# Early gate blocks two at a time in two banks, and the scores of a head's first two query blocks issued as one group

## The chip, the cores and the metric

One core of a Trainium2 chip runs the whole layer. The metric is the device time of one execution in microseconds (us), the median of several runs. The engines are named as the profile names them: PE is the matrix engine (PEld its weight loads), DVE the vector engine, ACT the scalar engine, POOL the GpSimd engine, SP the engine whose queue issues the DMAs.

## What is computed

One decoder layer on x of 1024 tokens by 1024 features, all in float32:

```python
h = rms_norm(x, norm_w)
proj = h @ w_in                                   # 1024 x 11296
q, k, v, z_a, xbc, z_s, dt_raw, gate_logits = split(proj)
# branch A: 8 heads, two softmax maps each, causal
p = softmax(where(causal, rms(q) @ rms(k).T / 8, -inf))
y_a = rms((p[0] - lam * p[1]) @ v) * silu(z_a)
# branch B: depthwise conv (4 taps) + silu on xbc, chunked state-space scan
# (32 heads, 4 groups, 8 chunks of 128), grouped rms norm of y * silu(z_s)
y_s = gated_group_rms_norm(ssd_chunked(...), z_s)
g_a, g_s = split(gate_logits)                     # 1024 + 1024
merged = sigmoid(g_a) * (y_a @ w_proj_attn) + sigmoid(g_s) * (y_s @ w_proj_ssd)
out = x + merged @ w_out
```

## The kernel before

Every large product is done in three matmuls of a reduced float format: each operand is split into a high and a low part (ACT rounds the high part, DVE or POOL subtracts it from the original to get the low part), and high x high, high x low and low x high add up in one PSUM bank. A weight tile is called `w` or, in a pair, `wp`; the two parts of the transposed h are `hH` and `hL`. There are eight PSUM banks, handed out by the slot list `trs`.

The program is written by a planner. Each piece of work is a Python generator; `Plan` keeps a modelled clock for PE (`pl.t`) and for each other engine, and always resumes the generator that is due first. The order of the instructions on each engine is the order in which the generators emit them. So a changed constant, modelled cost or table of order shifts instructions on all engines, while each engine executes its own in the written order and waits by semaphore for what is not ready.

The stages follow each other like this. **Front**: the table `FRONT_ORDER` is worked through item by item. `y0`, `y1` (tiles `pmz`) and `z..` (tiles `pz`) compute z_s; `c..` (tiles `fXc`, `fYc`, `fZc`) compute two column blocks of xbc each and their conv; `g..` (`fXg`, `fYg`, `fZg`) compute two column blocks of the gate logits; `d0` (`pdt`) computes dt. Items c, g and z are written as seven block products instead of eight; they read sums of blocks of h, the forms t1 to t4 (tiles `ft`), which ACT, DVE and POOL make from h during the first 100 us, and sums of weight blocks, which POOL makes (`rawf<-rawf,rawf`, `s<-rawf,rawf`) out of four raw tiles that have to be loaded together. The seven products of an item come in the order b11, t2, b21, t3, t1, t4, b22.

An `e` item (tile `pe`, function `gate_first`) computes the first 512 tokens of one gate block before the forms exist: 12 matmuls for the first half of the contraction, a copy of that partial sum by ACT (`gc`), which the later `g` item of the same number reads back from memory and then needs only five products, and 12 more matmuls into the same bank. The second 12 overwrite nothing, but PE has to wait for the copy before it adds to the bank. In the old order there are four `e` items (e6, e0, e4, e2), and each runs on its own.

**Attention and scan**: after the front come eight heads (`att_proj`, tiles `pma`, 192 matmuls each); the scan's chunks (`px`, `pc`, `pb`, `pS`, `pO`, `pD`, `py`) and the softmax blocks of the heads are woven in by the planner, a new chunk every `PACE` modelled us. The scores of a query block (`sc`, function `att_block`) contract over 64 rows: two maps are computed side by side on the two row halves of the array, three matmuls each, so a group is six matmuls; query block qb has 128 x (qb + 1) columns, in pieces of at most 512. `att_core` starts the four blocks of a half head one after the other, `SPACE` modelled us apart, and `STACK` sets how long after the last projection of the half the transposes of q and k are due. The intra-chunk products of the scan (`pO` or `pD`, output 64 x 64) use the array in column halves. `TURN` is the modelled cost of a change between such shapes.

**End**: the last four gate blocks (`pg`), then three block products with the projection weights (`px`, `py`, `pz` with `wp`), then the output product (`po..`).

`NEARLY` and `WPOOL` say for which weight tiles the low part is computed on POOL instead of DVE: from tile number `NEARLY` on, every `WPOOL`-th. `ZSUMS` sets when weight sums for z (`os`) are due.

Of the kernel before, what the change touches and what calls it, by code (L numbers as in the profile page):

```python
# [15 lines left out]
P = 128  # L16
S = 1024
D = 1024
KB = D // P
# [12 lines left out]
C_DT = 9216  # L32
C_GATE = 9248
NBIG, NW, NRAW, NMID, NSM = 17, 9, 4, 16, 8
PACE = 18.0
FRONT = 12
SLOW = 32.0
FRONT_ORDER = "y0 e6 y1 e0 e4 c6 e2 d0 c20 z06 c16 z07 z05 g0 c2 z04 c0 c10 z16 z03 g2 z17 z15 c4 z14 z13 c8 c14 g6 g8 c12 g4 g10 c22 c18"
REST = (("t2", 6), ("b22", 3), ("t3", 7), ("t1", 5), ("t4", 4))
ZSUMS = (75.0, 182.0, 3.0)  # L40
WPOOL = 3
NEARLY = 48
FINAL = (("b11", 1), ("t1", 5), ("t2", 6), ("t3", 7), ("b21", 2), ("b22", 3), ("t4", 4))
NFIN = 4 * len(FINAL)
HOP = 0.12
DONE = 0.2
STACK = 2.0
SPACE = 0.4
AHEAD = 0.2
DLAG = 1.5  # L50
TURN = 0.089
# [101 lines left out]
def tile_hybrid_layer(ctx: ExitStack, tc: tile.TileContext, x, norm_w, w_in, q_norm_w, k_norm_w,  # L153
# [35 lines left out]
    heads, abb = Share(bigs, 8), Share(bigs, 1)  # L189

    def bigt(shape, dt=F32, name="b"):
        return big.tile(shape, dt, tag="b4", name=name)
# [10 lines left out]
    def trt(name):  # L203
        return ps_tr.tile([P, 512], F32, tag="tr", name=name)
# [11 lines left out]
    def mm(o, lhsT, rhs, start, stop, after=0.0, **kw):  # L216
        nc.tensor.matmul(o, lhsT=lhsT, rhs=rhs, start=start, stop=stop, **kw)  # L217
# [16 lines left out]
    def pe_done():  # L234
        return pl.t + DONE
# [153 lines left out]
    PAIR_C = {"c": C_XBC, "g": C_GATE}  # L389
    for kind, i in ORDER1:  # L390
        if kind in PAIR_C:
            if kind == "g" and ("e", i) in ORDER1:
# [202 lines left out]
    def w_next(n):  # L595
        i = used[0]
        used[0] += n
        return list(range(i, i + n))

    def w_need(i):  # L600
        while i not in w_at:
            yield pl.t + 0.1
        while w_at[i] > pl.t:
            yield w_at[i]
# [285 lines left out]
            trs.give(k, t1)  # L890
        pl.spawn(att_core(h, half, (q, kq)), max(done))

    def att_core(h, half, q):
        for qb in range(half * 4, half * 4 + 4):
            while bigs.avail(1 + half) > pl.t:
                a = bigs.avail(1 + half)
                yield a if a < INF else pl.t + 0.2
            pk = [bigs.take() for _ in range(1 + half)]
            pl.spawn(att_block(h, qb, pk, q))
            yield pl.t + SPACE  # L900

    def att_block(h, qb, pk, q):
        v, zg, kk, ks = hd[h]
        q, kq = q
        n = (qb + 1) * P
        qsl = slice(qb % 4 * P, (qb % 4 + 1) * P)
        ex = []
        if qb < 4:
            pboth = bigt([P, 2, 512], name=f"p{h}{qb}")

        def soft(m):
            p = bigt([P, S], name=f"p{h}{qb}{m}") if qb >= 4 else pboth[:, m]
            nms, t1 = [], 0.0
            for i, (j, e) in enumerate(cols):
                while len(scs) <= i:
                    yield pl.t + 0.1
                sc, k, at = scs[i]
                at = max(at, t1 - HOP)
                yield at
                nms.append(tin(1, "nm"))  # L920
                nc.vector.tensor_tensor_reduce(out=p[:, j:e], in0=sc[m][:, 0:e - j], in1=maskb[:, S - n + j:S - n + e],  # L921
                                               scale=-1.0, scalar=nms[i - 1] if i else 3e38, op0=ALU.add, op1=ALU.min,
                                               accum_out=nms[i])
                t1 = pl.op("V", 0.08 + 1.042e-3 * (e - j), at)
                trs.give(k[m], t1)
# [6 lines left out]
        cols, scs, got = [(j, min(n, j + 512)) for j in range(0, n, 512)], [], {}  # L932
        for j, e in cols:
            k = yield from pl.get(trs, 2)
            sc = [trt(f"sc{h}{qb}{m}{j}") for m in range(2)]
            for n3, (a, b) in enumerate(((0, 0), (0, 1), (1, 0))):
                for m in range(2):
                    ms = slice(m * 64, m * 64 + 64)
                    mm(sc[m][:, 0:e - j], q[ms, a, qsl], kk[b][ms, j:e], n3 == 0, n3 == 2)
            scs.append((sc, k, pe_done()))  # L940
            if j == 0:
                for m in range(2):
                    pl.spawn(soft(m), pe_done())
        if qb % 4 == 3:
            bigs.give(kq, pl.t + 0.1)
        while len(ex) < 2:
            yield pl.t + 0.3
        pr, sums = zip(*[got[m] for m in range(2)])
# [240 lines left out]
            w_done(ids[n])  # L1189
            pl.spawn(step(b, p, into[p], cell, *how), pe_done())  # L1190

    g_c, g_first = {}, {i for kind, i in ORDER1 if kind == "e"}

    def gate_first(b):
        ids = w_next(2)
        k = yield from pl.get(trs, first=True)
        pm = mmt(f"pe{b}")
        for half in range(2):
            yield from w_need(ids[half])
            while half and ("g", b) not in g_c:  # L1200
                yield pl.t + 0.1
            for kb in range(half * 4, half * 4 + 4):
                yield from steps3(pm, blk(ids, kb), (hH[:, kb, 0:512], hL[:, kb, 0:512]), kb == 0, kb % 4 == 3, skip_group_check=True)
            w_done(ids[half])
            if half:
                pl.spawn(gate_evac(b, 0, pm, k), pe_done())
            else:
                pl.spawn(gate_copy(b, pm), pe_done())

    def gate_copy(b, pm):  # L1210
        at = pe_done()
# [1022 lines left out]
```

## Time and profile before

| what | us |
|---|---|
| runs | 1562.31, 1562.57, 1564.35 |
| median | 1562.57 |
| the profiled execution | 1562.57, its span 1560.8 |
| PE busy in it | 1540.5 |
| DVE, ACT, POOL busy | 1146.5, 894.3, 774.9 |

The profile shows one execution. A row of its timeline gives the start, the time until the end, the engine, the source line, the operation with output and inputs, the tile shape, and how many equal instructions were merged; in brackets stands the idle time before it and what ended it. Since nearly all matmuls go through one helper, all have the line L217, and tiles are told apart by name. Matmuls overlap: the distance between the starts of two of them says more about the cost of one than its own duration.

### The profile page before, as it was taken

What the parts mean: (1) busy time and instruction counts of PE and PEld (TensorE: products, weight loads), DVE (VectorE), ACT (ScalarE), POOL (GpSimd) and SP (SyncE); (2) the same over time, 40 slices, a digit from 0 to 9 for tenths busy, and PEclk for the clock granted to TensorE, in tenths of its full rate; (3) what the DMA queues carried; (4) which work ended last, traced back from release to release, by engine and by line L of the source; (5) the groups of instructions that cost most, each with busy time, mean ns of one, the idle gap of its engine ahead of it and who ended that gap; (6) DMA issues with size and microseconds to landing.
All of it is one profiled execution on the core that took longest, in us unless ns stands there. A gap on an engine that the chain in (4) does not pass through costs nothing.

```text
span 1560.8 us, 26193 instructions
## 1 busy us (share of the span) xinstructions
PE 1540.5 (99%) x8562; PEld 1252.8 (80%) x8562; DVE 1146.5 (73%) x2113; ACT 894.3 (57%) x2207; POOL 774.9 (50%) x900
## 2 busy tenths in 40 slices
PE   7999999999999999999999999999999999999999
PEld 5777888888888888888878888787878888888887
DVE  6778867757786587777777677776555577898985
ACT  7653435466566566666676677676556565352350
POOL 3274365344554544546586556464647745222005
PEclk9999999999999999999999999999999999999999
DMA  6576696876445542424454424253437598698846
GB/s 229 165 243 204 228 303 209 270 233 212 146 157 148 154 145 96 140 71 136 159 180 139 136 82 136 75 159 99 162 115 224 194 338 291 229 340 269 301 135 223
DMA packets 257130, 291.66 MB, mean 187 GB/s; under 512 B 18647, under 2 KB 162784, under 8 KB 256994
## 3 DMA queue, kind: packets, MB, share of 16 engines
q1 hardware_dynamic: 256990, 289.99, 57.3%
q8 instruction: 68, 1.11, 0.3%
q14 instruction: 68, 0.56, 0.1%
q10 hardware_dynamic: 4, 0.00, 0.0%
HBM read 198.57 MB, written 91.36 MB: 186 GB/s over the span
## 4 chain that ended last, share of the span: by engine, by line
PE 95%; DMA 1%; ACT 1%; DVE 1%; issue 0%; POOL 0%; SPq 0%; DVEq 0%; ACTq 0%; POOLq 0%
PE pma L217 23%; PE pz L217 11%; PE py L217 6%; PE fYc L217 6%; PE sc L217 4%; PE av L217 4%; PE fXc L217 4%; PE px L217 4%; PE fZc L217 4%; PE pO L217 3%; PE pg L217 3%; PE fYg L217 3%; PE pmz L217 2%; PE pa L231 2%; PE poz L217 1%; PE fZg L217 1%
## 5 line engine op out<-in xcount | busy, mean ns | idle before, releaser
L217 PE MATMUL pma<-w,hH 128*128 128x512 f32 x1024 | 344.9, 407 | 0.0
L217 PEld LDWEIGHTS pma<-w,hH 128*128 128x128 f32 x1024 | 186.2, 189 | 40.8 <-issue 6.6
L217 PE MATMUL pma<-w,hL 128*128 128x512 f32 x512 | 207.9, 406 | 0.0
L248 ACT ACTIVATE w<-raw 128x512 fp32r<-128x512 f32 (+1 forms) x166 | 100.9, 631 | 57.2 <-DMA raw<-wf_d 21.1
L256 DVE TENSOR_TENSOR w<-raw,w 128x512 fp32r<-128x512 f32 (+1 forms) x136 | 107.3, 808 | 29.0 <-ACT w L248 28.2
L217 PEld LDWEIGHTS pma<-w,hL 128*128 128x128 f32 x512 | 96.7, 189 | 20.3 <-issue 2.9
L217 PE MATMUL fYc<-ft,wp 128*128 128x512 f32 x432 | 106.1, 392 | 2.4 <-DVE ft L256 1.8
L248 ACT ACTIVATE p<-p,nm 128x256 f32<-128x256 f32 (+7 forms) x128 | 98.1, 770 | 17.8 <-DVE nm L921 15.9
L256 POOL TENSOR_TENSOR rawf<-rawf,rawf 128x512 f32<-128x512 f32 x54 | 71.8, 1329 | 64.2 <-issue 20.6
L217 PEld LDWEIGHTS fYc<-ft,wp 128*128 128x128 f32 x432 | 80.4, 188 | 20.4 <-DVE ft L256 2.2
L921 DVE CUSTOM_DVE_ANT_0 p<-sc,maskb 128x512 f32<-128x512 f32 (+3 forms) x128 | 69.3, 586 | 29.8 <-PE sc L217 28.3
L248 ACT ACTIVATE wp<-rawp 128x512 fp32r<-128x512 f32 x72 | 44.2, 627 | 81.7 <-PE py L217 23.5
L217 PE MATMUL pz<-w,ft 128*128 128x512 f32 x384 | 90.5, 392 | 0.3 <-DVE w L256 0.3
L256 POOL TENSOR_TENSOR os<-os,os 128x512 f32<-128x512 f32 x48 | 65.1, 1357 | 43.0 <-DMA os<-in_w_out_dram 19.5
L217 PEld LDWEIGHTS pz<-w,ft 128*128 128x128 f32 x384 | 71.6, 188 | 15.4 <-DVE w L256 0.7
L256 POOL TENSOR_TENSOR rawp<-rawp,rawp 128x512 f32<-128x512 f32 x36 | 53.2, 1491 | 53.8 <-DVE wp L256 40.1
L248 ACT ACTIVATE ab<-ab,nac 128x128 f32<-128x128 f32 x256 | 78.4, 397 | 2.2 <-POOL ab L1486 2.1
L217 PEld LDWEIGHTS av<-v,at 128*128 128x128 f32 x576 | 72.5, 191 | 5.1 <-issue 1.1
L288 POOL TENSOR_TENSOR rs<-rs,mhalf 128x4 f32<-128x4 f32 (+1 forms) x71 | 73.6, 1036 | 5.9
L248 ACT ACTIVATE wp<-rawf 128x512 fp32r<-128x512 f32 x100 | 60.3, 623 | 27.6 <-POOL rawf L256 24.1
L217 PE MATMUL av<-v,at 128*128 128x128 f32 x576 | 75.4, 276 | 0.0
L217 PE MATMUL sc<-kk,q 64*128 64x512 f32 (+3 forms) x576 | 70.8, 366 | 0.0
(367 smaller groups left out, 4144.6 us busy)
## 6 DMA issues: line engine op xcount, KB each, us to landing
raw<-in_w_in_dram SPq DMA_DIRECT2D x104, 256.0 KB, 3.2
rawf<-in_w_in_dram SPq DMA_DIRECT2D x72, 256.0 KB, 4.3
ab<-act_d SPq DMA_DIRECT2D x32, 512.0 KB, 4.7
wf_d<-os SPq DMA_DIRECT2D x48, 256.0 KB, 5.4
cv_d<-cv SPq DMA_DIRECT2D x48, 256.0 KB, 2.7
raw<-wf_d SPq DMA_DIRECT2D x48, 256.0 KB, 3.1
t_d<-ts SPq DMA_DIRECT2D x24, 512.0 KB, 2.6
os<-in_w_in_dram SPq DMA_DIRECT2D x32, 256.0 KB, 4.3
```

Source lines behind the costliest of these rows:

```text
L217: nc.tensor.matmul(o, lhsT=lhsT, rhs=rhs, start=start, stop=stop, **kw)
L231: nc.tensor.transpose(out=o, in_=i, identity=ident if idn is None else idn)
L248: nc.scalar.activation(o, i, f, **kw)
L256: (nc.vector if eng == "V" else nc.gpsimd).tensor_tensor(out=o, in0=a, in1=b, op=op)
L288: nc.gpsimd.tensor_tensor(out=dst, in0=dst, in1=mhalf[:, 0:cols], op=ALU.pow)
L921: nc.vector.tensor_tensor_reduce(out=p[:, j:e], in0=sc[m][:, 0:e - j], in1=maskb[:, S - n + j:S - n + e], scale=-1.0, scalar=nms[i - 1] if ...
```

## The change

Six things are changed together.

1. `FRONT_ORDER` has two `e` items instead of four. Each now does two gate blocks, b and b + 2, in two banks: first half of b, first half of b + 2, second half of b, second half of b + 2. The copy of b's partial sum by ACT falls in the time of the matmuls of b + 2. The weight list has the four tiles in the same order.
2. The front's table is reordered: the item right behind the second `e` item is now g8, then c6 and d0; before it was c6, then e2 and d0. The set of blocks computed is the same.
3. In `att_core` the scores of query blocks 0 and 1 are written together, twelve matmuls in a row, into one bank per map (block 0 in columns 0 to 127, block 1 in 128 to 383); the bank is given back when both blocks have been read. Blocks 2 and 3 follow without the distance `SPACE`.
4. The planner counts a change of shape as 0.189 or 0.159 instead of 0.089 modelled us, and `STACK` is 3.5 instead of 2.0.
5. `PACE` is 17.5 instead of 18.0; `ZSUMS` is moved.
6. `WPOOL` is 2 instead of 3 and `NEARLY` 39 instead of 48: in the whole program 52 weight tiles get their low part from POOL instead of 30, and 114 instead of 136 from DVE.

```diff
-PACE = 18.0
+PACE = 17.5
-FRONT_ORDER = "y0 e6 y1 e0 e4 c6 e2 d0 c20 z06 c16 z07 z05 g0 c2 z04 c0 c10 z16 z03 g2 z17 z15 c4 z14 z13 c8 c14 g6 g8 c12 g4 g10 c22 c18"
+FRONT_ORDER = "y0 e4 y1 e0 g8 c6 d0 c20 z06 c16 z07 c10 g0 c2 z05 z04 c0 z16 g6 z03 g2 z17 c4 z15 z13 z14 c8 c14 g4 c12 g10 c18 c22"
-ZSUMS = (75.0, 182.0, 3.0)
-WPOOL = 3
-NEARLY = 48
+ZSUMS = (83.0, 185.0, 9.0)
+WPOOL = 2
+NEARLY = 39
+HBUF = 8
-STACK = 2.0
+STACK = 3.5
...
-        c += TURN * (now != shape[0])
+        if now != shape[0]:
+            c += TURN + 0.1 if "r" in now + shape[0] else TURN + 0.07
...
         elif kind == "e":
-            wlist += block_w(w_in, KB, C_GATE + i * P)
+            for q in range(2):
+                for b in (i, i + 2):
+                    wlist.append(block_w(w_in, KB, C_GATE + b * P)[q])
...
+    def att_core(h, half, qk):
+        q, kq = qk
+        kk = hd[h][2]
+        for qbs in (((4,), (5,), (6,), (7,)) if half else ((0, 1), (2,), (3,))):
...
+            if len(qbs) == 2:
+                pieces = [[(0, 0, P, 0), (1, 0, 2 * P, P)]]
+            else:
+                pieces = [[(qbs[0], j, min(n, j + 512), 0)] for j in range(0, n, 512)]
+            for piece in pieces:
+                k = yield from pl.get(trs, 2)
+                sc = [trt(f"sc{h}{qbs[0]}{m}{piece[0][1]}") for m in range(2)]
+                users = [len(piece)] * 2
+                for qb, j, e, o in piece:
+                    qsl = slice(qb % 4 * P, (qb % 4 + 1) * P)
+                    for i, (a, b) in enumerate(((0, 0), (0, 1), (1, 0))):
+                        for m in range(2):
+                            ms = slice(m * 64, m * 64 + 64)
+                            mm(sc[m][:, o:o + e - j], q[ms, a, qsl], kk[b][ms, j:e], i == 0, i == 2, skip_group_check=True)
+                    cells[qb].append((sc, k, pe_done(), o, users))
+            if half:
+                yield pl.t + SPACE
...
     def gate_first(b):
-        ids = w_next(2)
-        k = yield from pl.get(trs, first=True)
-        pm = mmt(f"pe{b}")
+        ids = w_next(4)
+        pms = []
+        for g in (b, b + 2):
+            k = yield from pl.get(trs, first=True)
+            pms.append((mmt(f"pe{g}"), k))
         for half in range(2):
...
+            for n, (pm, k) in enumerate(pms):
+                g, i = b + 2 * n, ids[2 * half + n]
+                yield from w_need(i)
+                while half and ("g", g) not in g_c:
+                    yield pl.t + 0.1
```

How this moves instructions is seen at three places. The first is PE at the first `e` item (`pe6` and `pe4` are the banks of gate blocks 6 and 4, `w8` to `w10` weight tiles in order of use). Before:

```order
L217 MATMUL pe6_576<-hH_114,w8_381 128x512 x2
L217 MATMUL pe6_576<-hL_115,w8_381 128x512
L217 MATMUL pe6_576<-hH_114,w8_381 128x512
L217 MATMUL pe6_576<-hH_114,w9_488 128x512
L217 MATMUL pe6_576<-hL_115,w9_488 128x512
```

Now:

```order
L218 MATMUL pe4_576<-hH_114,w8_381 128x512
L218 MATMUL pe6_577<-hH_114,w9_488 128x512
L218 MATMUL pe6_577<-hL_115,w9_488 128x512
L218 MATMUL pe6_577<-hH_114,w9_488 128x512 x2
L218 MATMUL pe6_577<-hL_115,w9_488 128x512
L218 MATMUL pe6_577<-hH_114,w9_488 128x512 x2
L218 MATMUL pe6_577<-hL_115,w9_488 128x512
L218 MATMUL pe6_577<-hH_114,w9_488 128x512 x2
L218 MATMUL pe6_577<-hL_115,w9_488 128x512
L218 MATMUL pe6_577<-hH_114,w9_488 128x512
L218 MATMUL pe4_576<-hH_114,w10_510 128x512
```

The second half of a block used to stand right behind its first half; now the twelve matmuls of the other block stand between them.

The second place is PE at the scores of head 2 (`sc2000` and `sc2010` are the two maps of query block 0, `sc2100` and `sc2110` of block 1). Before:

```order
L217 MATMUL sc2000_8378<-kk20_7542,q20_8265 128x128
L217 MATMUL sc2010_8379<-kk20_7542,q20_8265 128x128
L217 MATMUL pma26_8371<-w100_6424,hH_114 128x512
L217 MATMUL pma26_8371<-w100_6424,hL_115 128x512
L231 MATMUL px22_8401<-ident_99,xr22_8326 128x128 x4
L217 MATMUL pma26_8371<-w101_7431,hH_114 128x512 x2
L217 MATMUL pma26_8371<-w101_7431,hL_115 128x512
L217 MATMUL pma26_8371<-w102_7463,hH_114 128x512
L217 MATMUL pO21_8293<-xdt21_8087,ab21_8122 64x64 x16
L217 MATMUL sc2100_8444<-kk20_7542,q20_8265 128x256
L217 MATMUL sc2110_8445<-kk20_7542,q20_8265 128x256
```

Now:

```order
L218 MATMUL sc2000_8297<-kk20_7499,q20_8218 128x128
L218 MATMUL sc2010_8298<-kk20_7499,q20_8218 128x128
L218 MATMUL sc2000_8297<-kk20_7499,q20_8218 128x256
L218 MATMUL sc2010_8298<-kk20_7499,q20_8218 128x256
L218 MATMUL sc2000_8297<-kk21_7500,q20_8218 128x256
L218 MATMUL sc2010_8298<-kk21_7500,q20_8218 128x256
L218 MATMUL sc2000_8297<-kk20_7499,q20_8218 128x256
L218 MATMUL sc2010_8298<-kk20_7499,q20_8218 128x256
L218 MATMUL sc2200_8311<-kk20_7499,q20_8218 128x384
```

Blocks 0 and 1 now follow each other, here with block 2 behind them. Counted over the whole order of PE, unbroken stretches of score matmuls go from 69 to 61: blocks 0 and 1 stood together in heads 0, 4, 6 and 7 already, and now do in all eight; the other joins come out of the new plan. A stretch of 64 x 64 scan products is followed directly by scores 7 times instead of 5. The set of matmuls on PE is the same, 7716.

The third place is DVE around the last parts of form t4 (`ft42`, `ft43`; `r217` is the input for the last 128 tokens; `fu6`, `fu7` and `fW6` are sums that read the banks of products 2, 4 and 5 of the running item). Before:

```order
L256 TENSOR_TENSOR fu7_1036<-fc_968,fYc6_939 128x512
L256 TENSOR_TENSOR w23_1041<-raw23_1008,w23_1041 128x512
L256 TENSOR_TENSOR w24_1057<-raw24_1010,w24_1057 128x512
L256 TENSOR_TENSOR w25_1063<-raw25_1022,w25_1063 128x4x32
L256 TENSOR_TENSOR fW6_1070<-fu7_1036,fZc6_940 128x512
L256 TENSOR_TENSOR w26_1068<-raw26_1031,w26_1068 128x4x32
L256 TENSOR_TENSOR ft42_906<-r216_746,ft40_904 128x2x128
L256 TENSOR_TENSOR ft43_907<-r216_746,ft41_905 128x2x128
L256 TENSOR_TENSOR ft42_906<-r217_728,ft40_904 128x2x128
L256 TENSOR_TENSOR ft43_907<-r217_728,ft41_905 128x2x128
```

Now:

```order
L258 TENSOR_TENSOR wp26_994<-rawf242_856,wp26_994 128x512
L258 TENSOR_TENSOR ft42_919<-r217_744,ft40_917 128x2x128
L258 TENSOR_TENSOR wp28_1011<-rawf241_855,wp28_1011 128x512
L258 TENSOR_TENSOR fu6_1037<-fc_1016,fYg8_984 128x512
L258 TENSOR_TENSOR ft43_920<-r217_744,ft41_918 128x2x128
L258 TENSOR_TENSOR fu7_1079<-fc_1016,fYg8_984 128x512
```

The last part of t4, which product 6 of the first item reads, stood behind the sum over product 5; it now stands behind the sum over product 2.

More of the change, by code (lines that the diff above doesn't have):

```diff
@@ L188, in tile_hybrid_layer @@
     qkm, atm, ytm, smids = Share(mids, 4), Share(mids, 4), Share(mids, 2), Share(mids, 10)
-    heads, abb = Share(bigs, 8), Share(bigs, 1)
+    heads, abb = Share(bigs, HBUF), Share(bigs, 1)
     def bigt(shape, dt=F32, name="b"):
@@ L391, in tile_hybrid_layer @@
         if kind in PAIR_C:
-            if kind == "g" and ("e", i) in ORDER1:
+            if kind == "g" and (("e", i) in ORDER1 or ("e", i - 2) in ORDER1):
                 short.add(len(wlist))
@@ L891, in qk_stack, with att_block @@
         pl.spawn(att_core(h, half, (q, kq)), max(done))
[L893 to L902, printed above, removed]
+    def att_core(h, half, qk):
+        q, kq = qk
+        kk = hd[h][2]
+        for qbs in (((4,), (5,), (6,), (7,)) if half else ((0, 1), (2,), (3,))):
+            cells = {}
+            for qb in qbs:
+                while bigs.avail(1 + half) > pl.t:
+                    a = bigs.avail(1 + half)
+                    yield a if a < INF else pl.t + 0.2
+                cells[qb] = []
+                pl.spawn(att_block(h, qb, [bigs.take() for _ in range(1 + half)], cells[qb]))
+            n = (qbs[-1] + 1) * P
+            if len(qbs) == 2:
[15 more added lines that the diff above has]
+                yield pl.t + SPACE
+        bigs.give(kq, pl.t + 0.1)
+    def att_block(h, qb, pk, scs):
         v, zg, kk, ks = hd[h]
-        q, kq = q
         n = (qb + 1) * P
-        qsl = slice(qb % 4 * P, (qb % 4 + 1) * P)
-        ex = []
+        ex, got = [], {}
+        cols = [(j, min(n, j + 512)) for j in range(0, n, 512)]
         if qb < 4:
@@ L916, in soft @@
                     yield pl.t + 0.1
-                sc, k, at = scs[i]
+                sc, k, at, o, users = scs[i]
                 at = max(at, t1 - HOP)
@@ L920, in soft @@
                 nms.append(tin(1, "nm"))
-                nc.vector.tensor_tensor_reduce(out=p[:, j:e], in0=sc[m][:, 0:e - j], in1=maskb[:, S - n + j:S - n + e],
+                nc.vector.tensor_tensor_reduce(out=p[:, j:e], in0=sc[m][:, o:o + e - j], in1=maskb[:, S - n + j:S - n + e],
                                                scale=-1.0, scalar=nms[i - 1] if i else 3e38, op0=ALU.add, op1=ALU.min,
@@ L924, in soft @@
                 t1 = pl.op("V", 0.08 + 1.042e-3 * (e - j), at)
-                trs.give(k[m], t1)
+                users[m] -= 1
+                if not users[m]:
+                    trs.give(k[m], t1)
             nm = nms[-1]
@@ L930, in soft @@
             got[m] = p, s_
[L932 to L945, printed above, removed]
+        for m in range(2):
+            pl.spawn(soft(m))
         while len(ex) < 2:
@@ L1190, in front_pair @@
             pl.spawn(step(b, p, into[p], cell, *how), pe_done())
-    g_c, g_first = {}, {i for kind, i in ORDER1 if kind == "e"}
+    g_c, g_first = {}, {j for kind, i in ORDER1 if kind == "e" for j in (i, i + 2)}
     def gate_first(b):
-        ids = w_next(2)
-        k = yield from pl.get(trs, first=True)
-        pm = mmt(f"pe{b}")
-        for half in range(2):
[L1199 to L1208, printed above, removed]
+        ids = w_next(4)
[3 more added lines that the diff above has]
+            pms.append((mmt(f"pe{g}"), k))
+        for half in range(2):
+            for n, (pm, k) in enumerate(pms):
[3 more added lines that the diff above has]
+                    yield pl.t + 0.1
+                for j in range(4):
+                    kb, w = half * 4 + j, wts[i]
+                    yield from steps3(pm, (w[:, 0, j, :], w[:, 1, j, :]), (hH[:, kb, 0:512], hL[:, kb, 0:512]), kb == 0, j == 3, skip_group_check=True)
+                w_done(i)
+                pl.spawn(gate_evac(g, 0, pm, k) if half else gate_copy(g, pm), pe_done())
     def gate_copy(b, pm):
```

## Prediction

> **What bounds the kernel now.** I read the page's head first, then the waits of PE alone, then the stage table.
>
> ```profile
> span 1560.8 us, 26193 instructions
> PE 1540.5 (99%) x8562; PEld 1252.8 (80%) x8562; DVE 1146.5 (73%) x2113; ACT 894.3 (57%) x2207; POOL 774.9 (50%) x900
> ```
>
> PE is busy for all but 20.3 us of the span, so the kernel is bound by what PE is given to do. A change can gain in two ways only: fewer of those 20.3 us, or the same matmuls in less time. The second is possible because a busy PE is not a PE at its peak. What PE waited for (columns: total, times, longest):
>
> ```profile
> PE pmz L217 <- ACT zc L248: 4.5, 2, 2.5
> PE pe L217 <- ACT gc L248: 2.9, 4, 0.7
> PE nwb L217 <- POOL one L2169: 2.7, 1, 2.7
> PE fYc L217 <- DVE ft L256: 1.8, 1, 1.8
> PE ph L231 <- DVE x L264: 1.7, 1, 1.7
> PE py L231 <- ACT xn L248: 0.9, 1, 0.9
> PE fYc L217 <- DVE fu L256: 0.7, 1, 0.7
> PE pod L217 <- DVE xr L264: 0.6, 1, 0.6
> PE fYg L217 <- DVE fu L256: 0.5, 1, 0.5
> PE pO L217 <- DVE ab L256: 0.5, 1, 0.5
> PE pz L217 <- DVE w L256: 0.3, 1, 0.3
> ```
>
> These are 17.1 us. The waits for `zc`, `one`, `x` and `xr` (9.5 us) lie at the start of the program and in its last product, where the order of PE is unchanged; they stay. In reach are `gc` (2.9), `ft` (1.8) and five small ones (2.9 together).
>
> **The change, part by part.** The matmuls are the same 7716, so only their neighbours and their waits count. The plain distance of two 512-column matmuls is 0.23 us, at the start of the first pair item for instance:
>
> ```profile
> 86.99 0.39 PE L217 MATMUL fXc<-hH,wp 128*128 128x512 f32 x1
> 87.22 0.39 PE L217 MATMUL fXc<-hL,wp 128*128 128x512 f32 x1
> ```
>
> *Gate blocks.* One of the four waits:
>
> ```profile
> 48.27 0.39 PE L217 MATMUL pe<-hH,w 128*128 128x512 f32 x1
> 49.35 0.50 PE L217 MATMUL pe<-hH,w 128*128 128x512 f32 x1 [0.69 <-ACT gc L248]
> 49.69 0.39 PE L217 MATMUL pe<-hL,w 128*128 128x512 f32 x1
> ```
>
> From 48.27 to 49.35 are 1.08 us instead of 0.23, and the next distance is 0.34, as PE refills: 0.85 + 0.11 = 0.96 us lost, more than the 0.69 that the wait shows. Four times make 3.9 us. In the new order twelve matmuls of the other block (12 x 0.23 = 2.7 us) stand where this wait was. The cover is enough if ACT reaches the copy within 2.7 - 0.85 = 1.9 us after the bank is complete. On ACT the copies stand behind a few form and weight roundings, so I take all of it: **-3.9**. Without cover (ACT late by more than 1.9 us each time) it would be 0.
>
> *Form t4.* Product 6 of the first pair item waited in its middle:
>
> ```profile
> 100.76 0.39 PE L217 MATMUL fYc<-ft,wp 128*128 128x512 f32 x1
> 102.91 0.73 PE L217 MATMUL fYc<-ft,wp 128*128 128x512 f32 x2 [1.76 <-DVE ft L256]
> ...
> 100.96 0.69 DVE L256 TENSOR_TENSOR fW<-fu,fZc 128x512 f32<-128x512 f32 x1 [0.29 <-PE fZc L217]
> 101.77 1.42 DVE L256 TENSOR_TENSOR ft<-r,ft 128x256 fp32r<-128x256 f32 x4
> ```
>
> The last four `ft` stood on DVE behind `fW`, which reads product 5 and so cannot start before 100.7. That is a wait made by the order, not by load: DVE had nothing to do for 0.29 us before `fW`. Now the last `ft` stands behind the sum over product 2, three products (3 x 12 x 0.23 = 8.2 us) ahead of product 6. The loss of 102.91 - 100.76 - 0.23 = 1.92 us goes: **-1.9**, bounds 0 and -1.9.
>
> *Scores.* A stretch of scores alone, then two blocks together, then block 1 alone:
>
> ```profile
> 775.11 0.40 PE L217 MATMUL pma<-w,hH 128*128 128x512 f32 x1
> 775.44 0.55 PE L217 MATMUL sc<-kk,q 64*128 64x128 f32 x6
> 775.92 0.51 PE L217 MATMUL pma<-w,hH 128*128 128x512 f32 x1
> 776.26 0.39 PE L217 MATMUL pma<-w,hL 128*128 128x512 f32 x1
> ...
> 608.94 0.96 PE L217 MATMUL sc<-kk,q 64*128 64x128 f32 x12
> 609.83 0.50 PE L217 MATMUL pma<-w,hH 128*128 128x512 f32 x1
> ...
> 691.12 0.62 PE L217 MATMUL sc<-kk,q 64*128 64x256 f32 x6
> 691.67 0.50 PE L217 MATMUL pO<-sh,ch 128*128 128x512 f32 x1
> ```
>
> Entering costs 775.44 - 775.11 - 0.23 = 0.10 us; leaving shows in the matmul after, 776.26 - 775.92 - 0.23 = 0.11. Inside, block 0 alone takes 0.48 and block 1 alone 0.55, together 1.03; the twelve in one stretch take 609.83 - 608.94 = 0.89, so 0.14 less. A join saves 0.10 + 0.11 + 0.14 = 0.35 us. Eight stretches fewer are 8 x 0.35 = **-2.8**. Bounds: the edges alone, 8 x 0.21 = -1.7, and 8 x 0.49 = -3.9 if the inner loss is twice this for wider blocks. Two more scan stretches that run directly into scores save one leaving and one entering each, 2 x 0.21 = **-0.4**. Only four of the eight joins are the edit itself; the other four hang on where the planner put the blocks, but as the order is fixed they count alike.
>
> *Two pair items back to back.* Now g8 is followed at once by c6, where e2 and d0 stood between before. A pair's four raw tiles are loaded when the pair before has released its own:
>
> ```profile
> 93.78 2.91 POOL L256 TENSOR_TENSOR wp<-rawf,wp 128x512 fp32r<-128x512 f32 x2
> ...
> 240.71 0.39 PE L217 MATMUL fXc<-hH,wp 128*128 128x512 f32 x1
> ...
> 245.64 2.22 SPq L277 DMA_DIRECT2D rawf<-in_w_in_dram  x4
> ...
> 258.49 0.68 DVE L256 TENSOR_TENSOR wp<-rawf,wp 128x512 fp32r<-128x512 f32 x1
> ...
> 259.75 0.39 PE L217 MATMUL fXc<-hH,wp 128*128 128x512 f32 x1
> ```
>
> The first pair released its last tile at 96.69, 9.7 us after its start at 86.99. In the later back-to-back pair, load issue to the end of the second weight's split took 259.17 - 245.64 = 13.5 us. Together the second weight would be ready 23.2 us after the first pair's start; PE needs it one pair (259.75 - 240.71 = 19.0) and one product (2.7) later, at 21.8. So up to 1.4 us is missing. On POOL the sums for z, which stood in the middle of the first pair's chain, now stand behind it, which brings the release forward by one or two of its 1.3 us steps. I take half, **+0.7**; bounds 0 and +2.8, if the second split is late for both of its weights.
>
> *Small waits and the moved constants.* `PACE`, `STACK`, `WPOOL` and the later start of the scan shuffle DVE, ACT and POOL but add no work to PE. The five small waits in reach are chance meetings in such a plan. I keep them at their 2.9 us, with bounds of -2.9 (all gone) and +2.9 (twice as many).
>
> **Sum**: -3.9 - 1.9 - 2.8 - 0.4 + 0.7 = -8.3 us. The profiled execution took 1562.57, which is also the median, its span 1560.8, and what lies around the span is not touched: 1562.57 - 8.3 = **1554.3 us**. Its own range, with the bounds of the terms only partly adding up, is 1551 to 1558.5.
>
> **Rivals.**
>
> *The front's weights come late (given back).* If c6, and the items behind it, meet their weights late by the full 2.8 us, and the loss recurs once, 5.6 us come in for the 0.7: 1554.3 + 4.9 = 1559.2, at the edge of no change. For it speaks that c6 follows at once in the densest part of the front; against it that two pairs stand back to back from 240.71 on and PE did not wait there.
>
> *The joined scores save nothing.* If the time inside a stretch is set by something else (the six weight loads), only the waits go: 1554.3 + 3.2 = 1557.5. Against it stand the rows at 608.94 and 775.44.
>
> *POOL holds up the heads' weights (slower).* Ten of the 22 low parts that move to POOL (32 instead of 22) belong to the heads, eight weights per head, read one after the other in its first block. Where POOL and DVE both subtract, both slow down:
>
> ```profile
> 797.27 1.65 POOL L256 TENSOR_TENSOR w<-raw,w 128x512 fp32r<-128x512 f32 x1
> ...
> 797.69 1.78 DVE L256 TENSOR_TENSOR w<-raw,w 128x512 fp32r<-128x512 f32 x1
> ...
> 801.39 0.71 PE L217 MATMUL pma<-w,hH 128*128 128x512 f32 x2
> ```
>
> The subtraction on DVE took 1.78 us here, where the one at 258.49 took 0.68, and this weight was ready at 799.47, 1.9 us before PE read it. Two more POOL subtractions queued ahead (2 x 1.3) and one such slowing (1.1) are 3.7 us, 1.8 more than the slack. At seven head starts that is 7 x 1.8 = 12.6: 1554.3 + 12.6 = 1567. It decides from 1.9 us of extra delay on, and only if every head start meets it. In the whole stage DVE has room:
>
> ```profile
> 600.00:800.00 200.00, 200.00 (x1376) 162.69 (x1374) 150.87 (x334) 137.24 (x436) 115.80 (x176) 1.00 0.42 128
> ```
>
> DVE (third figure) is busy for 150.87 of 200 us and POOL (fifth) for 115.80, so I give it little. [...]
>
> **How the numbers follow.** Forecast 0.68; weights late 0.15; scores save nothing 0.10; POOL slower 0.07. The time is that of the likeliest, 1554.3. The range goes from 1550.5 (the scores at -3.9, nothing lost between the pairs, and 2 of the 2.9 us of small waits gone: 1554.3 - 1.1 - 0.7 - 2.0) to 1561 (the late weights, with 1.8 us of new small waits beside them). A measurement of this kernel can tell about 0.2%, 3.1 us, from no change, so faster means below 1559.4: all of the forecast, of the scores' rival, and a little of the late weights: 0.81. Within 0.2%: the rest of that rival, 0.12. Slower: 0.07.
>
> **What would show it.** In the new profile's waits of PE there should be no row for `pe` on `gc` and none for product 6 on `ft` (both right: 5.8 us). Score rows at heads 1, 2, 3 and 5 should show x12 with about 0.9 us to the next matmul. The `zc`, `one` and `x` waits should stand as they are. A new wait of `fX` or `fY` on a weight at 108 to 125 us shows the first rival; waits of `pma` on `w` at head starts show the slower one. I am wrong as a whole if PE's idle time outside the first 40 us and the last product grows beyond today's.

## The result, and the profile after

The changed kernel takes 1553.1 us (median of six runs, 1552.03 to 1553.81). The kernel before took 1563.03 us in the same comparison, so the ratio is 0.9936, with a 95% interval of 0.9923 to 0.9948: about 10 us faster. Forecast were 1554.3 us, with a range of 1550.5 to 1561.0.

The head of the page of the changed kernel:

```profile
span 1550.0 us, 26098 instructions
PE 1534.9 (99%) x8562; PEld 1253.3 (81%) x8562; DVE 1131.5 (73%) x2091; ACT 887.6 (57%) x2203; POOL 806.9 (52%) x922
```

The span is 10.8 us shorter (the profiled execution is the shortest of the six). PE's idle time fell by 5.2 us (20.3 to 15.1) and its busy time by 5.6 (1540.5 to 1534.9), with the same 8562 matmuls and weight loads. So both ways to gain that the prediction named were used. What PE waited for now (total, times, longest):

```profile
PE pmz L218 <- ACT zc L250: 4.0, 2, 2.0
PE nwb L218 <- POOL one L2186: 2.7, 1, 2.7
PE ph L233 <- DVE x L266: 1.2, 1, 1.2
PE px L233 <- DVE cv L266: 1.1, 1, 1.1
PE pma L218 <- ACT at L250: 0.6, 1, 0.6
PE pod L218 <- DVE xr L266: 0.6, 1, 0.6
PE py L218 <- DVE u L258: 0.4, 1, 0.4
PE sc L218 <- DVE kk L258: 0.4, 1, 0.4
PE pO L218 <- DVE cT L258: 0.4, 1, 0.4
PE pq L233 <- DVE qk L258: 0.3, 1, 0.3
```

The rows for `gc`, `ft` and `fu` are gone. The waits of the start and of the last product (`zc`, `one`, `x`, `xr`) stand, in sum 8.5 us instead of 9.5, and a few small new ones came, the largest 1.1 us. The stage table (from : to, length, then PE, PEld, DVE, ACT, POOL busy with their instructions, granted clock, DMA share, GB/s) shows where the front got its time. Before:

```profile
40.00:80.00 40.00, 38.57 (x170) 31.25 (x168) 30.91 (x55) 25.62 (x56) 10.07 (x8) 1.00 0.54 169
80.00:120.00 40.00, 36.76 (x158) 27.57 (x157) 29.78 (x40) 19.27 (x40) 29.18 (x22) 1.00 0.73 243
```

After:

```profile
40.00:80.00 40.00, 40.00 (x178) 33.11 (x177) 29.21 (x51) 25.47 (x56) 9.69 (x8) 1.00 0.58 183
80.00:120.00 40.00, 40.00 (x178) 33.10 (x178) 21.40 (x32) 18.09 (x39) 29.80 (x23) 1.00 0.70 222
```

PE has no hole left between 40 and 120 us. The first copy of a gate block's partial sum, and the one behind it, in the timeline of ACT:

```profile
47.37 0.60 ACT L250 ACTIVATE gc<-pe 128x512 f32<-128x512 f32 x1 [1.22 <-PE pe L218]
...
50.09 0.60 ACT L250 ACTIVATE gc<-pe 128x512 f32<-128x512 f32 x1
```

The copy is done at 47.97. Twelve matmuls of the other block follow one another at 0.23 us, and PE comes back to the first bank at about 49.9 (47.17 + 12 x 0.227): 1.9 us to spare. ACT was ready for this copy before PE was, since it waited 1.22 us for the bank; at the other three the row shows no such wait. They leave 1.9, 1.7 and 0.9 us: the last copy ends at 84.34, and PE needs its bank at 85.25. Product 6 of the first pair, now g8, and the passage to c6 in the timeline of PE:

```profile
101.58 2.88 PE L218 MATMUL fYg<-ft,wp 128*128 128x512 f32 x12
104.30 0.39 PE L218 MATMUL fZg<-hH,wp 128*128 128x512 f32 x1
...
106.79 0.39 PE L218 MATMUL fZg<-hH,wp 128*128 128x512 f32 x1
107.02 0.39 PE L218 MATMUL fXc<-hH,wp 128*128 128x512 f32 x1
```

Twelve matmuls take 104.30 - 101.58 = 2.72 us, which is 12 x 0.227, without a break. The last `ft` on DVE had run from 94.28 to 94.75, 6.8 us before product 6 started. And c6 starts one plain distance behind g8, so its weights were there. Scores of blocks 0 and 1 in one stretch, and four blocks in one stretch:

```profile
674.85 0.96 PE L218 MATMUL sc<-kk,q 64*128 64x128 f32 x12
675.74 0.51 PE L218 MATMUL pma<-w,hH 128*128 128x512 f32 x1
...
593.38 2.17 PE L218 MATMUL sc<-kk,q 64*128 64x128 f32 x24
595.48 0.66 PE L233 MATMUL px<-ident,xr 128*128 128x128 f32 x4
```

The twelve take 0.89 us, as the one joint stretch of the kernel before did.

### The profile page after: what moved, and what is told of

It reads as the page before. It is cut to its first block, busy times and chain, and to the rows that moved or that the text cites. A ratio compares the mean times of both kernels' runs of the same rounds, so it can differ in the third digit from the quotient of the medians.

```text
span 1550.0 us, 26098 instructions
## 1 busy us (share of the span) xinstructions
PE 1534.9 (99%) x8562; PEld 1253.3 (81%) x8562; DVE 1131.5 (73%) x2091; ACT 887.6 (57%) x2203; POOL 806.9 (52%) x922
## 4 chain that ended last, share of the span: by engine, by line
PE 91%; POOL 2%; DVE 2%; ACT 2%; DMA 2%; issue 1%; SPq 0%; POOLq 0%; DVEq 0%; ACTq 0%
PE pma L218 21%; PE pz L218 11%; PE fYc L218 6%; PE py L218 5%; PE fXc L218 4%; PE sc L218 4%; PE fZc L218 4%; PE av L218 4%; PE fYg L218 3%; PE px L218 3%; PE pO L218 3%; PE pg L218 3%; PE pmz L218 2%; PE pa L233 2%; PE poz L218 1%; PE fZg L218 1%
## 5 line engine op out<-in xcount | busy, mean ns | idle before, releaser
L258 DVE TENSOR_TENSOR w<-raw,w 128x512 fp32r<-128x512 f32 (+1 forms) x114 | 91.0, 810 | 23.8 <-ACT w L250 23.6
L258 POOL TENSOR_TENSOR w<-raw,w 128x512 fp32r<-128x512 f32 x52 | 69.9, 1350 | 41.2 <-ACT w L250 41.2
L258 POOL TENSOR_TENSOR os<-os,os 128x512 f32<-128x512 f32 x48 | 68.9, 1436 | 13.4 <-DMA os<-in_w_in_dram 5.4
```

Of the source, the lines that this page charges most:

```text
L258: (nc.vector if eng == "V" else nc.gpsimd).tensor_tensor(out=o, in0=a, in1=b, op=op)
```

## The experiments

For the experiments I split PE's time from its first to its last matmul in the same way for every kernel, from the distances of matmul starts in the trace. **Waits** are the time by which a distance exceeds the plain one of that shape, where that is over 0.25 us; **half clock** is the time lost where the trace grants half the clock (told of in the last section); **net** is the rest. Stretches are runs of score matmuls in PE's written order. All times are us; the median is that of the timed runs, while the columns before it belong to the one execution that was traced. Each ratio below is to the kernel before as timed beside that kernel (medians from 1562.7 to 1563.9).

| kernel | stretches | waits to 40 | 40 to 440 | behind 440 | half clock | net | median |
|---|---|---|---|---|---|---|---|
| before | 69 | 6.0 | 8.5 | 1.3 | 0 | 1538.6 | 1563.0 |
| changed | 61 | 5.5 | 0 | 4.6 | 0 | 1533.6 | 1553.1 |
| e1 scores apart | 72 | 5.4 | 0 | 9.9 | 1.7 | 1539.0 | 1565.7 |
| e2 gates in turn | 62 | 5.8 | 4.5 | 12.0 | 5.1 | 1535.1 | 1570.4 |
| e3 less on POOL | 62 | 6.2 | 0 | 12.7 | 4.3 | 1534.3 | 1566.0 |
| e4 joined scores alone | 61 | 5.2 | 9.1 | 17.9 | 3.7 | 1535.5 | 1581.9 |
| e5 PACE 18 | 62 | 5.6 | 0 | 9.6 | 5.1 | 1533.8 | 1560.2 |
| e6 gates alone | 77 | 5.4 | 9.3 | 17.9 | 9.9 | 1540.3 | 1590.9 |
| e7 e2 ahead of c6 | 74 | 5.8 | 17.4 | 11.7 | 8.1 | 1541.0 | 1593.6 |
| e8 bunched scores | 47 | 5.4 | 0 | 8.2 | 1.7 | 1528.4 | 1553.4 |
| e9 before, PACE 17.5 | 74 | 6.0 | 9.1 | 11.6 | 1.7 | 1541.0 | 1576.6 |
| e10 old price of a change of shape | 69 | 6.3 | 0 | 9.0 | 1.7 | 1537.2 | 1562.4 |
| e11 bunched, PACE 17.25 | 48 | 7.1 | 0 | 21.2 | 7.6 | 1527.8 | 1569.7 |
| e12 bunched, PACE 17.75 | 45 | 5.6 | 0 | 9.7 | 4.0 | 1527.8 | 1555.1 |

The changed kernel's own gain reads from its first two rows: 8.5 us of waits in the front and 5.0 us of net time and 0.5 at the start are gone, 3.3 us of waits behind 440 us came: -10.7, against -10.8 in the span.

### e1: the scores of blocks 0 and 1 apart again

```diff
-        for qbs in (((4,), (5,), (6,), (7,)) if half else ((0, 1), (2,), (3,))):
+        for qbs in (((4,), (5,), (6,), (7,)) if half else ((0,), (1,), (2,), (3,))):
```

> The changed kernel with one thing undone: query blocks 0 and 1 get their scores separately again, each with banks of its own. Stretches of score matmuls go from 61 to 72, scan stretches that run directly into scores from 7 to 4. Theory of the prediction (a stretch costs 0.35 us, a direct passage saves 0.2): 1553.1 + 11 x 0.35 + 3 x 0.2 = 1557.6 us, PE's waits as in the changed kernel. Rival (the time inside a stretch hangs on something else, stretches are free): 1553.1.

Measured: 1565.7 us, ratio to the kernel before 1.0012 (1.0003 to 1.002). Both expectations are missed by 8 us and more. The net time alone behaves: 11 stretches more cost 5.4 us, 0.49 each, so the scores do not join for nothing. Nearly all the rest of the 12.6 us lies elsewhere: 5.3 us more waits behind 440 us and 1.7 us of half clock. The two largest of these waits:

```profile
PE pS L218 <- ACT at L250: 1.9, 1, 1.9
PE py L233 <- ACT w L250: 1.3, 1, 1.3
```

None of these tiles is a score. The planner wrote another order for all engines, and PE met other late operands.

### e2: the two gate blocks of an item one after the other

```diff
-        for half in range(2):
-            for n, (pm, k) in enumerate(pms):
+        for n, (pm, k) in enumerate(pms):
+            for half in range(2):
```

> The changed kernel, but in each e item the two blocks run one after the other (both halves of b, then both halves of b + 2), so that the second half stands right behind the first again; everything else in the table is as changed. Theory: the four waits of pe on gc come back at 0.96 us each, and the plan has one stretch more and two direct passages fewer: 1553.1 + 3.9 + 0.35 + 0.4 = 1557.7 us. Rival (the start of the front is held by weights and forms, so that PE would wait there in any case): 1553.9.

Measured: 1570.4 us, 1.0043 (1.003 to 1.0055); missed by 13 us. At its place the edit did what the prediction's term says, by PE's waits:

```profile
PE pe L218 <- ACT gc L250: 3.0, 4, 0.9
PE pO L218 <- DVE cv L266: 2.8, 1, 2.8
...
PE pO L218 <- DVE ab L258: 2.4, 1, 2.4
PE fYg L218 <- DVE fu L258: 2.0, 1, 2.0
```

The four waits for the copies are back, with 1.07 to 1.34 us between the two matmuls instead of 0.23. The other 13 us are mainly late operands at places that the edit does not touch, such as the rows below the first, and three times of half clock.

### e3: fewer weight low parts on POOL

```diff
-WPOOL = 2
-NEARLY = 39
+WPOOL = 3
+NEARLY = 48
```

> The changed kernel with WPOOL 3 and NEARLY 48 as before: 22 low parts go back from POOL to DVE. 62 stretches, 5 direct passages. Theory (POOL's share doesn't reach PE): 1553.1 + 0.35 + 0.4 = 1553.9 us. Rival 1 (DVE was relieved, and that is part of the gain): 1556 or more, with new waits of PE on DVE. [...]

Measured: 1566.0 us, 1.0015 (1.0006 to 1.0024). The time is on the side of the theory that POOL's share is needed, but its mechanism, PE waiting for DVE, is not what the trace shows. The longest wait, in the timelines of PE, then ACT, then POOL:

```profile
791.10 1.12 PE L233 MATMUL py<-ident,xn 128*128 128x128 f32 x4 [5.23 <-ACT xn L250]
...
790.33 0.72 ACT L250 ACTIVATE xn<-xn,rsy 128x512 f32<-128x512 f32 x1 [3.69 <-POOL rsy L290]
...
784.91 1.79 POOL L258 TENSOR_TENSOR ts<-ts,ts 128x512 f32<-128x512 f32 x1
786.78 1.26 POOL L258 TENSOR_TENSOR ts<-ts 128x512 f32<-128x512 f32 x1
...
789.25 1.04 POOL L290 TENSOR_TENSOR rsy<-rsy,mhalf 128x1 f32<-128x1 f32 x1
```

PE waited for ACT, ACT for `rsy`, a factor of one column, and that stood on POOL behind two sums of 512 columns and four short instructions. POOL had fewer weights to do here and was late all the same, by its order. What the share of POOL itself is worth stays open.

### e4: the joined scores alone, in the kernel before

```diff
-    def att_core(h, half, q):
-        for qb in range(half * 4, half * 4 + 4):
...
+    def att_core(h, half, qk):
+        q, kq = qk
+        kk = hd[h][2]
+        for qbs in (((4,), (5,), (6,), (7,)) if half else ((0, 1), (2,), (3,))):
...
```

The rest of the two functions is as in the changed kernel; tables, constants and gate items are those of before.

> The kernel before with only the new att_core and att_block: scores of blocks 0 and 1 joined, all constants, the table and the gate blocks as before. 61 stretches instead of 69, 5 direct passages as before. Theory: 1563.0 - 8 x 0.35 = 1560.2 us, the waits on gc and ft still there. Rival (stretches are free, the gain came from waits and constants): 1563.0.

Measured: 1581.9 us, 1.0118 (1.0103 to 1.0134): slower by 19 us than the kernel before, which neither theory allowed. Net time fell by 3.1 us for 8 stretches fewer, as it should. What came in is mainly one wait in the last product; PE's timeline and DVE's:

```profile
1498.18 4.17 PE L217 MATMUL poa<-w,hL 128*128 128x512 f32 x9 [8.19 <-DVE w L256]
...
1497.44 0.68 DVE L256 TENSOR_TENSOR w<-raw,w 128x512 fp32r<-128x512 f32 x1
```

DVE had no pause ahead of that row: some 20 sums of the merge (`gl`, `mm`, `pv`) at 0.6 us each were written ahead of one weight's low part. The same row, 8.2 us, appears in e6 and in e11 and in no other kernel.

After these four, the theory that a plan's time is the sum of local prices had failed four times, always upward. The next runs set it (theory A) against the one that every written order brings its own late operands (theory B).

### e5: one constant of the changed kernel set back

```diff
-PACE = 17.5
+PACE = 18.0
```

> The changed kernel with one constant set back: PACE 18.0 instead of 17.5. The matmuls are the same; the written order has 62 score stretches (61 in the changed kernel) and five direct passages between scan and score stretches (seven there). Theory A, the time is a sum of local prices (0.43 us for a stretch, 0.2 for a passage saved, the front's waits): 1553.1 + 0.4 + 0.4 = 1553.9, and PE waits in total within 3 us of the changed kernel's. Theory B, every new written order brings its own chance waits in scan, heads and end, and the changed kernel's order is one with few of them: 1556 to 1575, with at least 3 us more of waits on ACT or DVE behind 440 us, and a wait above 2.2 us, where there is one, with half the granted clock for about 3.4 us behind it. Both: no row of a wait of the gate blocks on their copies and none of product 6 on the last form.

Measured: 1560.2 us, 0.9982 (0.9972 to 0.9991). The total is that of theory B: net time is that of the changed kernel (1533.8 against 1533.6), waits behind 440 us are 5.0 us more, and 5.1 us are lost at half clock. The front is unharmed. Of the half clock, 1.7 us follow the wait for `zc` at 27.6 us, which every kernel has (see the last section). In this trace scan products run directly into scores three times, not five as expected, which moves theory A by 0.4 us. The 2.2 us named in theory B were an estimate and are no limit that the runs show: half clock followed the 2.9 us for `zc` here and 1.90 us in e1, and did not follow 2.87 us in e9.

### e6: the paired gate blocks alone, in the kernel before

```diff
-FRONT_ORDER = "y0 e6 y1 e0 e4 c6 e2 d0 c20 ..."
+FRONT_ORDER = "y0 e4 y1 e0 c6 d0 c20 ..."
...
-    g_c, g_first = {}, {i for kind, i in ORDER1 if kind == "e"}
+    g_c, g_first = {}, {j for kind, i in ORDER1 if kind == "e" for j in (i, i + 2)}
```

`gate_first` and its weight list are those of the changed kernel.

> The kernel before with the paired gate blocks alone (two e items instead of four, the rest of the front's table, the constants and the scores as before). 77 score stretches instead of 69, two direct passages instead of five; the last form still stands on DVE behind the sum over product 5. Theory A: 1563.0 - 3.9 (gate copies) + 8 x 0.43 + 3 x 0.2 = 1563.1. Theory B: as A plus 0 to 20 us of chance waits, so 1563 to 1583. Both: no wait of the gate blocks on their copies, and the wait of product 6 on the last form is there again with 1.5 to 2.2 us, which would show that this wait belongs to the place of the items in the table and not to the pairing.

Measured: 1590.9 us, 1.0175 (1.0156 to 1.0194), above even theory B. There is no wait for a copy any more. But the wait for the last form, which both theories expected, did not come back. In the kernel before, all four of the last `ft` stood on DVE behind `fW`. Here only one still does, in the timelines of DVE, then PE:

```profile
102.12 1.48 DVE L256 TENSOR_TENSOR ft<-r,ft 128x256 fp32r<-128x256 f32 x1
104.24 0.70 DVE L256 TENSOR_TENSOR fW<-fu,fZc 128x512 f32<-128x512 f32 x1 [0.63 <-PE fZc L217]
104.84 0.42 DVE L256 TENSOR_TENSOR ft<-r,ft 128x256 fp32r<-128x256 f32 x1
...
104.04 2.88 PE L217 MATMUL fYc<-ft,wp 128*128 128x512 f32 x12
```

With both pairs of gate blocks ahead of it c6 starts at 90.4 instead of 87.0 us. Product 6 runs from 104.04 without a break, although the last `ft` ends only at 105.26. So the wait hangs on how many of the forms still stand behind `fW`, four in the kernel before and one here.

Instead the front has two new waits above 2 us, in PE's timeline:

```profile
134.12 1.22 PE L217 MATMUL fYc<-ft,wp 128*128 128x512 f32 x2 [2.34 <-DVE fu L256]
...
147.73 1.19 PE L217 MATMUL pacum<-tv,tri 128*128 128x256 f32 x2 [4.31 <-DVE tv L264]
```

The stage in which they lie, in the stage table:

```profile
120.00:160.00 40.00, 33.35 (x134) 26.38 (x135) 35.15 (x58) 15.93 (x25) 18.11 (x16) 0.91 0.59 194
```

The same stage of the changed kernel:

```profile
120.00:160.00 40.00, 40.00 (x183) 30.68 (x181) 31.69 (x52) 14.93 (x26) 22.56 (x19) 1.00 0.65 209
```

`tv` is the chain that makes dt and its running sums out of d0; its steps stand on DVE between the sums `fu`, `fW` of the next pair and the conv of c6. DVE is busy for 35.15 of 40 us there, against 31.69 in the changed kernel, where g8 stands ahead of c6 and d0 and the weights go to POOL more often. Which of the two lightens DVE enough is not shown by this run; e3, with the new table and the old POOL share, has no front wait, which speaks for the table.

### e7: e2 ahead of c6 in the kernel before

```diff
-FRONT_ORDER = "y0 e6 y1 e0 e4 c6 e2 d0 c20 ..."
+FRONT_ORDER = "y0 e6 y1 e0 e4 e2 c6 d0 c20 ..."
```

> The kernel before with one entry of the front's table moved: e2 ahead of c6 instead of behind it (four single gate blocks, all constants and the scores as before). 74 score stretches instead of 69, one direct passage instead of five. The last form now stands on DVE ahead of the sum over product 5. Theory A: 1563.0 - 1.9 + 5 x 0.43 + 4 x 0.2 = 1564.1. Theory B: as A plus 0 to 20 us. Both: the wait of product 6 on the last form is gone or below 0.4 us, and the four waits of the gate blocks on their copies stay at 2.5 to 3.5 us in sum.

Measured: 1593.6 us, 1.0193 (1.0165 to 1.022), again above theory B. PE's waits:

```profile
PE fYg L217 <- DVE fu L256: 5.5, 3, 2.2
...
PE pz L217 <- ACT w L248: 3.3, 2, 2.5
PE pe L217 <- ACT gc L248: 2.8, 4, 0.7
```

The wait for the last form is gone and the four waits for the copies stand, as expected of the place. The 1.9 us that this wins are lost many times over between 140 and 154 us, where PE waits for the dt chain and for the weights of `pz`, while DVE and ACT also have the conv to do, and in the gate pairs later (`fYg`).

### e8: score pieces written two at a time

```diff
-            for piece in pieces:
-                k = yield from pl.get(trs, 2)
+            for g in range(0, len(pieces), 2):
+                bunch = pieces[g:g + 2]
+                ks = yield from pl.get(trs, 2 * len(bunch))
+                for u, piece in enumerate(bunch):
+                    k = ks[2 * u:2 * u + 2]
```

> The changed kernel with the pieces of a head's scores written two at a time (four banks taken at once), so 47 score stretches instead of 61 and two direct passages instead of seven; all else as in the changed kernel. Theory A: 1553.1 - 14 x 0.43 + 5 x 0.2 = 1548.1, waits as in the changed kernel. Theory B: 1548 to 1568 by the chance waits of the new order, with PE busy time falling by about 5 us whatever the waits do. A rival to the price of a stretch (stretches cost nothing, waits alone decide): 1553.1 and PE busy time unchanged at 1535. Taking four banks at once could make PE wait for banks: then waits of sc on ACT or DVE rows appear.

Measured: 1553.4 us, 0.9943 (0.9925 to 0.996), the same as the changed kernel. The busy line of its page:

```profile
PE 1532.6 (99%) x8562; PEld 1254.4 (81%) x8562; DVE 1133.9 (73%) x2091; ACT 889.4 (57%) x2203; POOL 805.2 (52%) x922
```

and the largest of PE's waits behind the start:

```profile
PE py L233 <- ACT xn L250: 2.4, 3, 1.3
```

That stretches cost nothing is refuted: net time fell by 5.2 us, 0.37 for each of the 14 stretches. It was given back as 3.6 us of waits behind 440 us and 1.7 us of half clock. The half clock is not the work of the bunched scores: it starts at 26.1 us, behind a wait that all kernels have. PE's busy time fell by 2.3 us (1534.9 to 1532.6) and not by the 5 expected; 1.7 of the difference is the half clock, which counts as busy (in e1 3.41 of 3.41 us at a granted clock of 0.50). No row shows `sc` waiting for a bank.

### e9: one constant of the kernel before moved

```diff
-PACE = 18.0
+PACE = 17.5
```

> The kernel before with one constant moved: PACE 17.5 instead of 18.0, nothing else. 74 score stretches instead of 69, five direct passages as before. Theory A (sum of local prices): 1563.0 + 5 x 0.43 = 1565.2, within 3 us. Theory B (the kernel before is itself one of the written orders with few chance waits, and another order costs up to 30 us more, in the waits and in the half clock behind the long ones): 1568 to 1593. Both: the four waits of the gate blocks on their copies stay at 2.5 to 3.5 us.

Measured: 1576.6 us, 1.008 (1.0063 to 1.0097). Theory B: a constant that adds no work costs the kernel before 12.8 us (1563.9 beside it). In the traced execution it is 14.9: 2.4 us of net time for five more stretches, 10.8 of waits and 1.7 at half clock. The waits for copies and for the last form are unchanged in PE's waits:

```profile
PE pe L217 <- ACT gc L248: 2.9, 4, 0.7
...
PE fYc L217 <- DVE ft L256: 1.8, 1, 1.8
```

### e10: the planner's old price of a change of shape

```diff
-            c += TURN + 0.1 if "r" in now + shape[0] else TURN + 0.07
+            c += TURN
```

> The changed kernel with only the planner's price of a change of shape set back to 0.089. 69 score stretches instead of 61, four direct passages instead of seven; the matmuls, tables and other constants as in the changed kernel. Theory A: 1553.1 + 8 x 0.43 + 3 x 0.2 = 1557.1, PE busy time up by some 4 us. Theory B: 1557 to 1577, with at least 3 us more of waits behind 440 us than in the changed kernel.

Measured: 1562.4 us, 0.9993 (0.9984 to 1.0003). The total lies in theory B's range, and so do the waits (4.4 us more behind 440); the 1.7 us of half clock follow the wait at 27.7 us that all kernels have. The net time is 3.6 us higher for eight stretches more, as both said. So the price in the planner's model is worth as many stretches as the whole gain in them from before to after, although the edit of `att_core` is in both kernels.

### e11 and e12: two more orders of the bunched scores

```diff
-PACE = 17.5
+PACE = 17.25        (e11; in e12 17.75)
```

> The kernel with score pieces written two at a time (47 stretches, 1553.4 us, with 3.6 us more waits than the changed kernel), PACE 17.25 instead of 17.5: 48 stretches and six or seven direct passages. Theory A: 1553.1 - 13 x 0.43 = 1547.5. Theory B: 1547 to 1567 by chance waits, so as likely above 1553 as below.

> The same with PACE 17.75: 45 stretches, three direct passages. Theory A: 1553.1 - 16 x 0.43 + 4 x 0.2 = 1547.0. Theory B: 1547 to 1567 by chance waits, so as likely above 1553 as below.

Measured: 1569.7 us, 1.0037 (1.0024 to 1.0051), and 1555.1 us, 0.9941 (0.9926 to 0.9956). Their net times are the lowest of all (1527.8) and their waits are not; e11 lies above theory B's range, with the 8.2 us of e4 in the last product. None of the twelve is faster than the changed kernel. Bunched scores with its waits would by the net times be some 5 us faster, an estimate that no run here reaches.

## Why the prediction was right

**Gate blocks (-3.9): right.** The four waits are gone in the changed kernel and come back in e2 with the same size. In the changed kernel 0.9 to 1.9 us are to spare at each copy.

**Form t4 (-1.9): right in place and size.** e6 and e7 add that it needs neither g8 nor, in e7, the pairing; in both, more gate blocks ahead of c6 were enough. But in the old table that same step comes with 9.3 and 17.4 us of front waits (in e7 some 3.5 of them the gate copies), so the gain can't be had from this step alone: all eight kernels that have the new table with the interleaved gate blocks (the changed kernel, e1, e3, e5, e8, e10, e11, e12) have no front wait over 0.25 us.

**Scores (-2.8): right in mechanism, too small; direct passages (-0.4): open.** The step that was mis-sized is the 0.35 us for a join, taken from one pair of rows. Over all 14 kernels net time is 1507.3 + 0.443 x stretches (standard error 0.02), with 45 to 77 stretches and no kernel further from this than 1.2 us; pairs of kernels give 0.37 (e8) to 0.49 (e1). Eight joins are 3.5 us. The rows show where the difference lies. Counted as in the prediction (entering, leaving, and the time inside beyond plain streaming), a stretch costs 0.62 us for the 24 at 593.38, 0.52 for the six of block 0 alone at 631.92, 0.43 for the six of block 1 at 637.54 and 0.44 for the twelve 512-column ones at 647.47. So joining block 1 to block 0 saves 0.35, but joining two wide pieces saves all of the second stretch, 0.42. Whether direct passages need a term of their own the fit can't tell: added to it they get about zero with a standard error of 0.14 each. The rest of the 5.0 us of net time is the longer distance behind the waits that are gone (0.34 instead of 0.23 us at 49.35 in the kernel before, so six times about 0.11) and about 0.8 that the split does not explain.

**Two pair items back to back (+0.7): did not come.** c6 started 0.23 us behind g8. The first rival (weights late) went with it, and the second (scores save nothing) is refuted by e1, e4 and e8. POOL holding up the heads' weights did not happen either: there is no row of `pma` on `w`.

**Small waits (kept at 2.9, bounds +-2.9): right by luck in its size.** The waits behind 440 us went from 1.3 to 4.6 us, and those of `fu`, `ab`, `w` and `xn` in the front (3.0 us together) went away, so the sum held. That the total came within 1.2 us of the forecast rests on this luck. As a bound for a new order it is far too narrow. Twelve other orders have 8.2 to 21.2 us behind 440 us, which is 3.6 to 16.6 more than the changed kernel, and three constants alone (e5, e9, e10) gave 5.0, 10.3 and 4.4 us more than the kernel they start from. The prediction treated the two orders' chance waits as alike. It had not priced that one of these waits can be 8.2 us long (e4, e6, e11), nor that half the granted clock can follow a wait (1.90 us in e1, with 1.7 us more lost behind it).

So the result is right for reasons that hold, the front's waits and fewer stretches, with the condition that the new order's late operands are few. Why the two orders shown first have so few and the twelve written for the experiments so many is not settled by these runs. An obvious rival, that these two were picked by their time out of many such orders while the twelve were not, is not tested. Nor is it settled which of the constants it hangs on: the three settings of the changed kernel that were moved alone or as a pair (`PACE`, the price of a change of shape, `WPOOL` with `NEARLY`) all made it worse.

## What to carry to other kernels

Where a planner writes the order of all engines, price an edit at its place (the waits it removes, the stretches it joins) and give the new order a bound of its own, taken from what another order of the same work costs, here 0 to 30 us; an experiment that undoes one part measures the new order as much as the part, so read its rows and not its total. A stretch of score matmuls, which have another shape than their neighbours, cost 0.43 to 0.52 us here for six matmuls and 0.62 for 24, beyond plain streaming. PE's waits were worth keeping below some 1.5 us here: a wait could cost its length and 1.7 us more in these traces, the shortest single one of 1.6 us (`sc` on `at` in e7), while half clock followed none of the 92 windows of 3.41 us with 0.7 to 1.55 us idle.

## What the runs showed of the hardware

**Behind some waits the granted clock was 0.50, for 3.41 us or two or three times that.** In e1 PE waited 1.90 us. The stage table around it:

```profile
744.10:747.51 3.41, 1.51 (x8) 0.95 (x7) 0.42 (x1) 3.41 (x14) 1.42 (x4) 1.00 0.97 339
747.51:750.92 3.41, 3.41 (x12) 2.73 (x11) 2.93 (x5) 0.69 (x2) 3.12 (x4) 0.50 0.04 14
```

Behind the wait the granted clock is 0.50 (third figure from the end), PE issues 12 matmuls in a time that holds 23 and 24 at full clock (740.69 to 744.10 and 750.92 to 754.34), and two 512-column matmuls are 0.43 us apart (748.53 and 748.96) instead of 0.23. That costs 1.7 us more (half of 3.41). In e9 no half clock followed a longer wait; first its row in PE's timeline, then the stage table around it:

```profile
761.87 1.83 PE L217 MATMUL av<-v,at 128*128 128x128 f32 x14 [2.87 <-ACT at L248]
```

```profile
756.60:760.01 3.41, 2.40 (x17) 1.79 (x15) 0.00 (x0) 3.41 (x10) 3.11 (x3) 1.00 0.00 0
760.01:763.43 3.42, 1.56 (x14) 1.56 (x15) 0.00 (x0) 3.42 (x11) 1.94 (x3) 1.00 0.38 153
763.43:766.84 3.41, 3.41 (x22) 2.99 (x21) 2.60 (x7) 1.50 (x10) 3.17 (x7) 1.00 0.32 93
```

The times at half clock, but for the one behind the last matmul, are 3.41, 6.83 or 10.24 us long in every trace, and within one execution all their starts lie a whole number of 3.413 us apart (to 0.003 us). In the kernel before and the changed one the full clock is on record for 1546.24 and 1536.00 us, which is 453 and 450 times 3.4133. So I cut each trace into windows on that grid and took PE's idle time in each, the window less PE's busy figure. Of 19 full-speed windows with 2.0 us idle or more, 18 were followed by a window at half clock; of 22 with 1.55 to 2.0 us, 11; of 92 with 0.7 to 1.55 us, none. e1's wait put 1.90 us into one window; e9's was split 1.0 and 1.9 over two, and the second of these stayed without effect. So some 60% of a window idle was followed by half clock in all but one case, and it came behind single waits of 1.6 (e7) to 2.9 us (e5).

In the fourteen traced executions between 0 and 9.9 us were lost so; the two without any loss are those of the kernel before and the changed one. This belongs in part to the execution and not to the kernel. All fourteen wait 2.0 to 3.3 us for `zc` at 26 to 29 us; in eight of them (e3 to e6, e8, e10 to e12) half clock follows there, in six not, among these e9 with 2.9 us. And the 48 executions of the kernel before that were timed beside the experiments have mean granted clocks from 0.997 to 1.000: the 15 at 1.000 take 1562.3 us on average, the 11 at 0.998 take 1564.1.
